# Scaling q and k in place through a tree of block factors in an HGRN2 mixer, and writing TensorE's order in both mixers out by hand

## The chip, the cores and the metric

The kernel runs on one core of a Trainium2 chip. The metric is the time of one execution on the device, in microseconds (us). A core has TensorE (PE; its weight loads are listed as PEld), VectorE (DVE), ScalarE (ACT), GpSimd (POOL) and SyncE (SP, which here only issues transfers). Each engine takes its own instructions in the order in which they stand in its queue, and an instruction that waits for another engine holds up all that stands behind it in its queue.

## The reference

A trunk of four layers over 256 positions of 1024 values. Layers 0 and 3 mix the positions by differential attention, layer 1 by a gated recurrence (HGRN2), layer 2 by a gated MLP. Behind its mixer every layer attends to 256 memory positions and runs a feed-forward block. Cut to the two mixers:

```python
def diff_attention(h, ...):
    q, k, v = jnp.split(h @ w_in, 3, axis=-1)      # 8 heads, 2 x 64 for q and k, 128 for v
    logits = einsum('bqhcd,bkhcd->bhcqk', q, k) * scale + bias, -inf above the diagonal
    p = softmax(logits)
    attn = p[:, :, 0] - lam * p[:, :, 1]
    o = einsum('bhqk,bkhd->bqhd', attn, v)
    return (rmsnorm(o, subln_g) * (1.0 - lam_init)) @ w_out

def hgrn2(h, ...):
    q, f, i, g = jnp.split(h @ w_in, 4, axis=-1)   # 8 heads of 128
    log_f = log(lb + (1 - lb) * sigmoid(f))        # the decay of each position
    key = 1.0 - exp(log_f); qf = silu(q)
    # A[t, s] = sum_k qf[t,k] key[s,k] * (product of the decays of s+1 .. t at k), s <= t
    o = A @ i
    return (rmsnorm(o, onorm_g) * silu(g)) @ w_out
```

## The kernel before

All products with weights are made of three matmuls, since fp32 operands are split into a high and a low part. SP loads weights into three buffers (`wraw`); ScalarE casts the high part (`whi`, line 127), VectorE subtracts it to get the low part (`wlo`, line 128), three units ahead of TensorE's use. `columns_block` writes products transposed, 256 output columns (a unit, 32 matmuls in 16 pairs of lines 197 and 201) at a time, for q, k and HGRN's f; `join` (lines 212 and 213) adds its two halves on ScalarE and VectorE and frees two of the four accumulator banks of PSUM. `rows_block` (line 159) makes v and g. Four further banks (`ps`) are shared by everything small.

In the attention, for each of four head pairs: the logits (line 529), bias and maximum (534, 538), the exps (544), a factor `dco` from the sums (550, 551), the difference `de` (554), and its transposes for the product with v (559, 562). A head pair needs the unit of q of its number. In layer 0 `memory()` also loads and normalises the memory (lines 384 to 394) and transposes it (`pst`, 239) into `m`. In HGRN a triangle of 256 positions is cut into levels of doubling blocks: for each level GpSimd multiplies keys by decay products (`ke`, line 696) and extends these (`hs`, 703), VectorE does the like for q (`qe`, 693, and 700), TensorE multiplies them (`psa`, 715 and 726), and VectorE copies the level's blocks into the triangle `A` by a mask (717). The levels' masks hold the diagonal too.

What sets the order: the Python loops issue everything in program order, and a scheduler then places the instructions on each engine's queue as it expects operands to come. So TensorE's attention and levels lie among the projections where the scheduler puts them.

## Time and profile before

| | |
|---|---|
| median of 3 runs | 1650.75 us (1649.39 to 1651.85) |
| the profiled execution | 1651.97 us, span 1650.3 us |
| PE busy | 1614.3 us, 98% |
| DVE, ACT, POOL busy | 1035.8 us (63%), 875.0 us (53%), 83.8 us (5%) |
| layer 0's attention, first logits to last output matmul | 73.92 to 121.87 |
| HGRN, first diagonal matmul to the end of the levels | 483.15 to 531.63 |
| layer 3's attention | 1286.59 to 1331.46 |

A matmul's row in the timeline carries the time to its modelled end, which overlaps the next one's start; its pace is the difference of two starts. An "x" and a number says how many of a kind follow one another. A bracket at the end of a row gives the idle time before it, and what ended it. In names, an arrow points from the inputs to the output.

### The profile page before, as it was taken

The numbers are of one execution on the slowest core, as the hardware profiler recorded it, in microseconds if no ns is written. First come the engines' busy times: TensorE is split into PE (matmuls) and PEld (weight loads), VectorE is DVE, ScalarE is ACT, GpSimd is POOL, SyncE is SP. The second block draws the span as 40 slices with busy tenths as digits, with TensorE's granted clock in tenths as the row PEclk, the third lists the DMA queues.
The fourth block names the chain that finished last, engine by engine and source line by source line (L and its number), as shares of the span: only waits on it lengthen the run. The fifth ranks groups of instructions, "written<-read, shape, count | busy, mean of one in ns | idle before, by whom it ended". The sixth has DMA issues, their size and how long they took to land.

```text
span 1650.3 us, 21291 instructions
## 1 busy us (share of the span) xinstructions
PE 1614.3 (98%) x8221; PEld 1358.9 (82%) x8221; DVE 1035.8 (63%) x1466; ACT 875.0 (53%) x1451; POOL 83.8 (5%) x104
## 2 busy tenths in 40 slices
PE   7799999999998999999999999999999999999998
PEld 6678888888887888888888888888888788888886
DVE  6687665554689567655545866555547876655453
ACT  5576554453552666554436556544435675554452
POOL 2000000000037000000000000000000000000000
PEclk9899999999999999999999999999999999999999
DMA  8644445546640655455565654555656445455461
GB/s 271 211 134 153 155 153 187 193 164 202 185 141 28 204 178 171 145 193 167 195 213 166 193 185 148 164 179 165 217 182 202 143 138 179 143 184 195 130 233 71
DMA packets 151291, 283.04 MB, mean 172 GB/s; under 512 B 6267, under 2 KB 79894, under 8 KB 151062
## 3 DMA queue, kind: packets, MB, share of 16 engines
q1 hardware_dynamic: 146384, 274.82, 50.7%
q10 hardware_dynamic: 4806, 6.87, 1.4%
q8 instruction: 64, 1.05, 0.3%
q14 instruction: 37, 0.30, 0.1%
HBM read 280.60 MB, written 2.63 MB: 172 GB/s over the span
## 4 chain that ended last, share of the span: by engine, by line
PE 85%; DVE 5%; POOL 3%; ACT 3%; DMA 2%; issue 2%; POOLq 0%; DVEq 0%; ACTq 0%
PE acc L159 63%; PE acc L197 10%; PE acc L201 5%; PE pst L239 3%; PE pso L889 1%; PE psl L850 1%; DVE wlo L128 1%; POOL ke L696 1%; POOL hs L703 1%; ACT de L544 1%; DMA mem<-in_mem_dram 1%; PE pl L529 1%; ACT junk L262 1%; ACT whi L127 1%; DMA x<-in_x_dram 1%
## 5 line engine op out<-in xcount | busy, mean ns | idle before, releaser
L128 DVE TENSOR_TENSOR wlo<-wraw,whi 128x1024 fp32r<-128x1024 f32 (+1 forms) x536 | 637.4, 1196 | 457.2 <-ACT whi L127 453.8
L127 ACT CAST whi<-wraw 128x1024 fp32r<-128x1024 f32 (+1 forms) x536 | 547.3, 1026 | 535.2 <-PE acc L159 464.2
L159 PE MATMUL acc<-whi,xs 128*128 128x512 f32 x1728 | 542.9, 392 | 0.7 <-DVE hf L213 0.7
L159 PEld LDWEIGHTS acc<-whi,xs 128*128 128x128 f32 x1728 | 324.1, 188 | 69.0 <-DVE hf L213 1.5
L159 PE MATMUL acc<-wlo,xs 128*128 128x512 f32 x864 | 337.9, 391 | 0.0
L197 PE MATMUL acc<-xs,whi 128*128 128x512 f32 x704 | 248.8, 398 | 0.0
L201 PE MATMUL acc<-xs,wlo 128*128 128x256 f32 x704 | 196.9, 283 | 0.0
L159 PEld LDWEIGHTS acc<-wlo,xs 128*128 128x128 f32 x864 | 162.4, 188 | 33.2 <-issue 1.0
L197 PEld LDWEIGHTS acc<-xs,whi 128*128 128x128 f32 x704 | 132.4, 189 | 29.0
L159 PE MATMUL acc<-wlo,hh 128*128 128x512 f32 x352 | 137.3, 390 | 0.0
L159 PE MATMUL acc<-whi,hh 128*128 128x512 f32 x352 | 137.3, 392 | 0.0
L201 PEld LDWEIGHTS acc<-xs,wlo 128*128 128x128 f32 x704 | 133.8, 190 | 0.9
L159 PE MATMUL acc<-whi,hl 128*128 128x512 f32 x352 | 111.9, 390 | 0.0
L159 PE MATMUL acc<-whi,oh 128*128 128x512 f32 x256 | 100.2, 391 | 1.7 <-DVE bt L213 1.7
L159 PE MATMUL acc<-wlo,oh 128*128 128x512 f32 x256 | 100.5, 393 | 0.0
L197 PE MATMUL acc<-m,whi 128*128 128x512 f32 x256 | 90.3, 395 | 0.0
L159 PE MATMUL acc<-whi,ol 128*128 128x512 f32 x256 | 84.8, 392 | 0.0
L159 PE MATMUL acc<-whi,m 128*128 128x512 f32 x256 | 80.7, 391 | 0.0
L159 PEld LDWEIGHTS acc<-whi,hh 128*128 128x128 f32 x352 | 66.1, 188 | 14.5 <-DVE ftmp L916 1.1
L159 PEld LDWEIGHTS acc<-whi,hl 128*128 128x128 f32 x352 | 66.1, 188 | 13.7
L159 PEld LDWEIGHTS acc<-wlo,hh 128*128 128x128 f32 x352 | 66.1, 188 | 13.4
L201 PE MATMUL acc<-m,wlo 128*128 128x256 f32 x256 | 72.1, 282 | 0.0
(223 smaller groups left out, 1760.9 us busy)
## 6 DMA issues: line engine op xcount, KB each, us to landing
wraw<-in_ffn_w_gu_dram SPq DMA_DIRECT2D x160, 512.0 KB, 4.5
wraw<-in_ffn_w_down_dram SPq DMA_DIRECT2D x44, 1024.0 KB, 4.9
wraw<-in_ca_w_kv_dram SPq DMA_DIRECT2D x32, 1024.0 KB, 5.2
wraw<-in_da_w_in_dram SPq DMA_DIRECT2D x24, 1024.0 KB, 6.9
wraw<-in_ca_w_q_dram SPq DMA_DIRECT2D x16, 1024.0 KB, 5.2
wraw<-in_ca_w_o_dram SPq DMA_DIRECT2D x16, 1024.0 KB, 4.9
wraw<-in_hg_w_in_dram SPq DMA_DIRECT2D x16, 1024.0 KB, 5.5
wraw<-in_da_w_out_dram SPq DMA_DIRECT2D x8, 1024.0 KB, 4.9
```

The source lines that it names most:

```text
L127: nc.scalar.copy(h, rq)
L128: nc.vector.tensor_tensor(l, rq, h.bitcast(F32), op=ALU.subtract)
L159: nc.tensor.matmul(acc[key], lhsT=x_(k)[:, t * P : (t + 1) * P], rhs=w_[kk][:, 0, c], start=first and j == 0, stop=last and j == 2,)
L197: nc.tensor.matmul(acc[j].rearrange("p (s t) -> p s t", s=2), lhsT=wh[k // 4][:, k % 4, c], rhs=x[:, :, k, :], start=k == 0, stop=False, s ...
L201: nc.tensor.matmul(acc[j][:, 0:256], lhsT=wl[k // 4][:, k % 4, c], rhs=x[:, 0, k, :], start=False, stop=k == 7, skip_group_check=True,)
L239: nc.tensor.transpose(ps[:, i * 256 + t * P : i * 256 + (t + 1) * P], src[:, t, cs * P : (cs + 1) * P], self.ident)
L262: self.nc.scalar.activation(junk[:, : src.shape[1]], src, AF.Square, accum_out=acc)
L529: nc.tensor.matmul(lg[c][:, i * w : (i + 1) * w], lhsT=qt[r, 2 * hp + i, t * P : (t + 1) * P], rhs=kt[r, 2 * hp + i, 0:w], start=True, sto ...
L544: nc.scalar.activation(e[t][:, c, i], e[t][:, c, i], AF.Exp, bias=mx[:, t, k : k + 1], accum_out=sm[:, t, c, i : i + 1])
L696: nc.gpsimd.tensor_tensor(kev[:, :, 0, :], kv[:, :, 0, :], sv[:, :, 0, :], op=ALU.mult)
L703: nc.gpsimd.tensor_tensor(sv[:, :, 0, :], sv[:, :, 0, :], sv[:, :, 1, 0:1].to_broadcast([P, 4 * nb, half]), op=ALU.mult)
L850: nc.tensor.matmul(ps[:, t * 256 : (t + 1) * 256], lhsT=q_[:, 2 * h + d, t * P : (t + 1) * P], rhs=k_[:, 2 * h + d, :], start=n == 0, stop ...
```

## The change

Four things are done.

1. The blocks become generators (`columns_steps`, `rows_steps`) that yield behind each matmul; `advance(filler, n)` issues n more of them. In the mixers, a written list says after how many projection matmuls each piece of attention (`weigh`: logits to `de`; `turn`: its transposes) or each level stands, and `in_order()` makes TensorE keep this order. The other engines are still placed by the scheduler.
2. In HGRN, `hks` holds the key times the next position's decay, and it and q are multiplied in place, level by level, with a tree of block products `bl` (`hb` in the trace) on VectorE. GpSimd's products, `qe`, `ke` and the copy of f are gone.
3. The diagonal is made apart: 16 matmuls of one column each (`psd`) sum q times key, and ScalarE scales the identity by them into `A`.
4. The masks lose their diagonal.

The functions named `weigh` and `turn` have the bodies of the former loop.

```diff
-        self.columns_block(self.xs, done_q)
...
-        for hp in range(4):
+
+        def both():
+            yield from self.columns_steps(self.xs, done_q)
+            yield from self.rows_steps(xh, xl, 8, done_v)
+
+        filler = both()
+        order = self.in_order()
+        order.__enter__()
+
+        def weigh(hp):
...
+            return e
+
+        def turn(hp, e):
+            hs = slice(2 * hp, 2 * hp + 2)
...
-        self.rows_block(xh, xl, 8, done_v)
+        es = {}
+        for n, act, hp in (
+            (44, weigh, 0), (24, weigh, 1), (24, turn, 0), (16, weigh, 2),
+            (20, turn, 1), (12, weigh, 3), (24, turn, 2), (24, turn, 3),
+        ):
+            advance(filler, n)
+            if act is weigh:
+                es[hp] = weigh(hp)
+            else:
+                turn(hp, es.pop(hp))
+        advance(filler, 224)
+        order.__exit__(None, None, None)
...
-            nc.vector.tensor_scalar(kk[:, 2 * b : 2 * b + 2, :], fs, -1.0, 1.0, op0=ALU.mult, op1=ALU.add)
-            nc.vector.tensor_copy(sx[:, 2 * b : 2 * b + 2, 0:255], fs[:, :, 1:256])
+            c = slice(2 * b, 2 * b + 2)
+            nc.vector.tensor_scalar(kk[:, c, :], fs, -1.0, 1.0, op0=ALU.mult, op1=ALU.add)
+            nc.vector.tensor_tensor(ks[:, c, 0:255], kk[:, c, 0:255], fs[:, :, 1:256], op=ALU.mult)
+            nc.vector.tensor_tensor(qk[:, c, :], q[:, c, :], kk[:, c, :], op=ALU.mult)
...
-        self.columns_block(self.xs, done_f)
-
-
-
-        qes = self.slab(4, [P, 2, 8, P], name="qe")
-        ke = self.slab(13, [P, 8, 256], name="ke")
...
-        nc.gpsimd.memset(A, 0.0)
-        nc.gpsimd.memset(f.rearrange("p h (b s) -> p (h b) s", s=2)[:, :, 0:1], 1.0)
-        first = lambda x: x.rearrange("p h (t n) -> p h t n", t=2)[:, :, :, 0]
...
-        ps = self.ps("psd")
-        nc.tensor.matmul(ps[:, 0:16], lhsT=self.ones, rhs=qk.rearrange("p h t -> p (h t)"), start=True, stop=True)
-        nc.scalar.copy(A[0:1, :, :, 0].rearrange("p t h -> p h t"), ps[0:1, 0:16].rearrange("p (h t) -> p h t", h=8))
-        for lev in range(8):
...
+        def diagonal(hq):
+            ps = self.ps("psd")
+            dg = self.small([P, 8], "hdg", bufs=2)
+            for i in range(4):
+                for t in range(2):
+                    nc.tensor.matmul(
+                        ps[:, 2 * i + t : 2 * i + t + 1], lhsT=qk[:, hq * 4 + i, t * P : (t + 1) * P],
+                        rhs=self.ones[:, 0:1], start=True, stop=True,
+                    )
+            nc.vector.tensor_copy(dg, ps[:, 0:8])
+            for i in range(4):
+                for t in range(2):
+                    nc.scalar.mul(A[:, t, hq * 4 + i, :], self.ident, dg[:, 2 * i + t : 2 * i + t + 1])
...
+            if lev == 0:
+                f2 = f[:, hs, 1:255].rearrange("p h (b s) -> p h b s", s=2)
+                nc.vector.tensor_tensor(bl[1][:, hs, 0:127], f2[:, :, :, 0], f2[:, :, :, 1], op=ALU.mult)
+            else:
+                b2 = bl[lev][:, hs].rearrange("p h (b s) -> p h b s", s=2)
+                nc.vector.tensor_tensor(bl[lev + 1][:, hs], b2[:, :, :, 0], b2[:, :, :, 1], op=ALU.mult)
+            ps = self.ps("psa")
+            for t in range(2):
+                for i in range(4):
+                    h = hq * 4 + i
+                    o = t * 256 + i * 64
+                    right = q[:, h, t * P : (t + 1) * P].rearrange("p (b s e) -> p b s e", s=2, e=half)[:, :, 1, :]
...
-                nc.gpsimd.tensor_tensor(kev[:, :, 0, :], kv[:, :, 0, :], sv[:, :, 0, :], op=ALU.mult)
...
-                        nc.vector.tensor_tensor(
-                            fv[:, :, 1, :], fv[:, :, 1, :], sv[:, :, 0, 0:1].to_broadcast([P, 4 * nb, half]), op=ALU.mult
...
-                    nc.gpsimd.tensor_tensor(
-                        sv[:, :, 0, :], sv[:, :, 0, :], sv[:, :, 1, 0:1].to_broadcast([P, 4 * nb, half]), op=ALU.mult
...
+            else:
+                for x, s in ((qv, 1), (kv, 0)):
+                    flat = x.rearrange("p h b s e -> p (h b) s e")[:, :, s, :]
+                    by = bl[lev][:, hs].rearrange("p h (b s) -> p (h b) s", s=2)[:, :, 1 - s : 2 - s]
+                    nc.vector.tensor_tensor(flat, flat, by.to_broadcast([P, 4 * nb, half]), op=ALU.mult)
...
+        def both():
+            yield from self.columns_steps(self.xs, done_f)
+            yield from self.rows_steps(xh, xl, 8, done_v)
+            yield from self.rows_steps(xh, xl, 8, done_g)
+
+        filler = both()
+        with self.in_order():
+            advance(filler, 88)
+            diagonal(0)
+            advance(filler, 12)
+            level(0, 0)
+            advance(filler, 22)
+            level(1, 0)
+            advance(filler, 30)
+            diagonal(1)
+            advance(filler, 8)
+            for i in range(14):
+                level(*((i // 2, 1) if i % 2 == 0 else (2 + i // 2, 0)) if i < 12 else (i - 6, 1))
+                advance(filler, 9 if i < 11 else 17)
+            advance(filler, 320)
```

The step that lets the other blocks run between:

```diff
@@ -198,13 +221,17 @@
                         acc[j].rearrange("p (s t) -> p s t", s=2), lhsT=wh[k // 4][:, k % 4, c], rhs=x[:, :, k, :],
                         start=k == 0, stop=False, skip_group_check=True,
                     )
+                    yield
                     nc.tensor.matmul(
                         acc[j][:, 0:256], lhsT=wl[k // 4][:, k % 4, c], rhs=x[:, 0, k, :],
                         start=False, stop=k == 7, skip_group_check=True,
                     )
+                    if k < 7 or j == 0:
+                        yield
             if mid is not None and u == at:
                 mid()
             done(u, acc)
+            yield
```

TensorE in layer 0, before, around the transposes of the memory (`pst<-ident,mem`) and q's projection (`acc`), of which 83 matmuls stand ahead of the first transpose:

```order
L197 MATMUL acc<-xs,whi 128x512
L201 MATMUL acc<-xs,wlo 128x256
L197 MATMUL acc<-xs,whi 128x512
L239 MATMUL pst<-ident,mem 128x128 x4
L201 MATMUL acc<-xs,wlo 128x256
L197 MATMUL acc<-xs,whi 128x512
L239 MATMUL pst<-ident,mem 128x128 x12
L201 MATMUL acc<-xs,wlo 128x256
L197 MATMUL acc<-xs,whi 128x512
L201 MATMUL acc<-xs,wlo 128x256
```

The same place after the change; 44 matmuls of q stand ahead, and the first logits (`pl`) directly behind:

```order
L220 MATMUL acc<-xs,whi 128x512
L225 MATMUL acc<-xs,wlo 128x256
L220 MATMUL acc<-xs,whi 128x512
L225 MATMUL acc<-xs,wlo 128x256
L266 MATMUL pst<-ident,mem 128x128 x16
L563 MATMUL pl_606<-dk,dq 128x128
L563 MATMUL pl_607<-dk,dq 128x128
L563 MATMUL pl_606<-dk,dq 128x128
L563 MATMUL pl_607<-dk,dq 128x128
L563 MATMUL pl_619<-dk,dq 128x256
L563 MATMUL pl_620<-dk,dq 128x256
L563 MATMUL pl_619<-dk,dq 128x256
L563 MATMUL pl_620<-dk,dq 128x256
```

The transposes moved up by 39 matmuls, and stand as one piece between q's first part and the logits.

ScalarE in layer 0, before, from the load of the memory to its squares (`junk`):

```order
L384 DMA mem<-in_mem_dram 128x2x1024
L127 CAST whi<-wraw 128x1024
L212 COPY dq<-acc 128x256 x2
L127 CAST whi<-wraw 128x1024
L262 ACTIVATE junk,ss<-mem 128x512
L127 CAST whi<-wraw 128x1024
L262 ACTIVATE junk,ss<-mem 128x512
L212 COPY dq<-acc 128x256
```

And after; `bias<-tbd` is the load of the attention's bias:

```order
L411 DMA mem<-in_mem_dram 128x2x1024
L641 DMA bias<-tbd 128x8x256
L289 ACTIVATE junk,ss<-mem 128x512
L131 CAST whi<-wraw 128x1024
L289 ACTIVATE junk,ss<-mem 128x512
L239 COPY dq<-acc 128x256
L289 ACTIVATE junk,ss<-mem 128x512
L239 COPY dq<-acc 128x256
```

The casts and joins between the memory's load and its first use moved behind that use, and the bias load ahead of it.

VectorE in layer 3, before, through the first head pair's softmax (`dq<-acc,dq` is a join of q):

```order
L213 TENSOR_TENSOR dq<-acc,dq 128x256
L534 SCALAR_TENSOR_TENSOR de<-pl_10613,dsc,bias 128x256
L534 SCALAR_TENSOR_TENSOR de<-pl_10614,dsc,bias 128x256
L213 TENSOR_TENSOR dq<-acc,dq 128x256
L538 TENSOR_REDUCE dmx<-de 128x4
L534 SCALAR_TENSOR_TENSOR de<-pl_10626,dsc,bias 128x512
L534 SCALAR_TENSOR_TENSOR de<-pl_10627,dsc,bias 128x512
L128 TENSOR_TENSOR wlo<-wraw,whi 128x1024
L538 TENSOR_REDUCE dmx<-de 128x4
L128 TENSOR_TENSOR wlo<-wraw,whi 128x1024
L548 COPY ds_10609<-dsm 128x4
L608 RECIPROCAL hrs<-ds_10609 128x4
```

And after the change, through the same softmax and the next joins:

```order
L572 TENSOR_REDUCE dmx<-de 128x4
L568 SCALAR_TENSOR_TENSOR de<-pl_10522,dsc,bias 128x512
L568 SCALAR_TENSOR_TENSOR de<-pl_10523,dsc,bias 128x512
L572 TENSOR_REDUCE dmx<-de 128x4
L582 COPY ds_10431<-dsm 128x4
L657 RECIPROCAL hrs<-ds_10431 128x4
L584 RECIPROCAL dco<-dsm 128x4
L585 SCALAR_TENSOR_TENSOR dco<-dco,lam,ds_10431 128x4
L240 TENSOR_TENSOR dq<-acc,dq 128x256
L588 SCALAR_TENSOR_TENSOR de<-de,dco 128x128 x2
L588 SCALAR_TENSOR_TENSOR de<-de,dco 128x256 x2
L240 TENSOR_TENSOR dq<-acc,dq 128x256
```

Two joins of q moved from ahead of the softmax to behind `dco`, the second also behind the four updates of `de`, and the weight subtractions from inside the softmax to behind it.

VectorE in HGRN, before, at the end of the f block and the first level:

```order
L658 TENSOR_SCALAR hk<-hf 128x512
L659 COPY hs<-hf 128x2x255
L680 TENSOR_TENSOR qk<-hq,hk 128x16
L128 TENSOR_TENSOR wlo<-wraw,whi 128x1024
L693 TENSOR_TENSOR qe<-hq,hf 128x512
L717 COPY_PREDICATED hA<-masks,psa 128x256 x2
L700 TENSOR_TENSOR hf<-hf,hs 128x256x2
L717 COPY_PREDICATED hA<-masks,psa 128x256 x2
L717 COPY_PREDICATED hA<-masks,psa 128x128x2 x2
L693 TENSOR_TENSOR qe<-hq,hf 128x512 x2
```

And after, in the f block's third quarter, where the block factors (`hb`) and the products for the diagonal (`hqk`) are made:

```order
L721 TENSOR_TENSOR hqk<-hq,hk 128x512
L712 TENSOR_TENSOR hf<-hf,rb 128x512
L132 TENSOR_TENSOR wlo<-wraw,whi 128x1024
L715 TENSOR_SCALAR hf<-hf,lb 128x256 x2
L132 TENSOR_TENSOR wlo<-wraw,whi 128x1024
L719 TENSOR_SCALAR hk<-hf 128x512
L760 TENSOR_TENSOR hb<-hf 128x4x127
L720 TENSOR_TENSOR hks<-hk,hf 128x2x255
L721 TENSOR_TENSOR hqk<-hq,hk 128x512
L763 TENSOR_TENSOR hb<-hb 128x256
L742 COPY hdg<-psd 128x8
```

The products with f moved from the levels into the f block's own time, between the weight subtractions.

## Rows read from the trace of the kernel before

**Rows 1.** The page: the span, and TensorE's busy time, its share and instructions.
```profile
span 1650.3 us, 21291 instructions
...
PE 1614.3 (98%) x8221; PEld 1358.9 (82%) x8221; DVE 1035.8 (63%) x1466; ACT 875.0 (53%) x1451; POOL 83.8 (5%) x104
```

**Rows 2.** TensorE's waits: line, releaser, total us, times, longest.
```profile
PE pst L239 <- DVE mem L394: 9.5, 1, 9.5
PE pst L239 <- DMA x<-in_x_dram: 5.8, 3, 4.0
```

**Rows 3.** Windows: stretch, length, busy us of PE, PEld, DVE, ACT, POOL, clock, DMA.
```profile
73.90:121.90 48.00, 47.48 (x279) 38.31 (x278) 39.87 (x76) 36.37 (x112) 1.01 (x1) 1.00 0.47 150
483.00:531.60 48.60, 43.56 (x303) 37.99 (x301) 47.76 (x57) 10.36 (x20) 42.20 (x29) 1.00 0.03 10
1286.60:1331.50 44.90, 43.40 (x256) 34.46 (x255) 37.54 (x72) 35.34 (x109) 1.01 (x1) 1.00 0.39 128
```

**Rows 4.** Timeline of TensorE in layer 0: start, us, line, operation [idle <-releaser].
```profile
38.11 0.40 PE L197 MATMUL acc<-xs,whi 128*128 128x512 f32 x1
...
51.98 0.40 PE L197 MATMUL acc<-xs,whi 128*128 128x512 f32 x1
...
61.85 1.11 PE L239 MATMUL pst<-ident,mem 128*128 128x128 f32 x4 [9.47 <-DVE mem L394]
...
62.62 0.56 PE L201 MATMUL acc<-xs,wlo 128*128 128x256 f32 x1
```

**Rows 5.** Timeline of TensorE in layer 3's attention.
```profile
1286.59 1.58 PE L529 MATMUL pl<-dk,dq 64*128 64x128 f32 x16
...
1289.13 0.85 PE L159 MATMUL acc<-whi,xs 128*128 128x512 f32 x3
...
1290.50 0.84 PE L159 MATMUL acc<-whi,xs 128*128 128x512 f32 x3
...
1297.17 1.87 PE L529 MATMUL pl<-dk,dq 64*128 64x128 f32 x16
```

**Rows 6.** Timeline of TensorE at the start of HGRN's levels.
```profile
483.15 0.37 PE L682 MATMUL psd<-qk,ones 128*128 128x16 f32 x2
483.37 1.98 PE L715 MATMUL psa<-hq,ke 128*128 128x64 f32 x16
485.15 0.48 PE L159 MATMUL acc<-whi,xs 128*128 128x512 f32 x1
```

**Rows 7.** Timeline of ScalarE around the memory's load; ACTq marks a DMA issue.
```profile
42.47 0.41 ACTq L384 DMA_DIRECT2D mem<-in_mem_dram  x1
...
55.79 0.63 ACT L262 ACTIVATE junk<-mem 128x512 bf16<-128x512 f32 x1 [10.34 <-DMA mem<-in_mem_dram]
...
64.92 0.47 ACT L228 ACTIVATE m<-pst,G 128x256 fp32r<-128x256 f32 x1 [0.17 <-PE pst L239]
```

**Rows 8.** Timeline of SyncE: weight loads issued in that time.
```profile
46.16 18.97 SPq L111 DMA_DIRECT2D wraw<-in_da_w_in_dram  x3
```

**Rows 9.** Timeline of VectorE behind the memory's normalisation.
```profile
62.37 2.35 DVE L128 TENSOR_TENSOR wlo<-wraw,whi 128x1024 fp32r<-128x1024 f32 x2
```

**Rows 10.** Timeline of VectorE in layer 3: a join, and the softmax's end.
```profile
1288.13 0.42 DVE L213 TENSOR_TENSOR dq<-acc,dq 128x256 f32<-128x256 f32 x1
...
1294.86 0.18 DVE L550 RECIPROCAL dco<-dsm 128x4 f32<-128x4 f32 x1 [0.60 <-ACT de L544]
...
1295.34 1.41 DVE L554 SCALAR_TENSOR_TENSOR de<-de,dco 128x128 f32<-128x128 f32 x4
```

**Rows 11.** Timeline of VectorE in HGRN's f block: one line twice.
```profile
468.36 0.68 DVE L652 TENSOR_TENSOR hf<-hf,rb 128x512 f32<-128x512 f32 x1
...
473.32 1.57 DVE L652 TENSOR_TENSOR hf<-hf,rb 128x512 f32<-128x512 f32 x1
```

**Rows 12.** Windows with TensorE's clock: after the two longest waits (columns as rows 3).
```profile
12.00:14.00 2.00, 2.00 (x9) 1.70 (x9) 1.95 (x2) 1.62 (x5) 0.00 (x0) 1.00 1.06 347
58.00:66.00 8.00, 4.15 (x19) 3.97 (x20) 6.45 (x11) 6.04 (x13) 0.70 (x1) 0.50 0.45 134
```

More of the change, by code (lines that the diff above doesn't have):

```diff
@@ L59, in level_masks, with advance @@
         t = np.array([t for t in range(P) if t // half % 2 == 1])[None, :]
-        left = (s // (2 * half) == t // (2 * half)) & (s // half % 2 == 0)
-        out.append(left | ((s == t) & (t % half == 0)))
+        out.append((s // (2 * half) == t // (2 * half)) & (s // half % 2 == 0))
     return np.ascontiguousarray(np.stack(out, 1).astype(np.float32))
+def advance(gen, n):
+    for _ in range(n):
+        next(gen, None)
 class Trunk:
@@ L139, in next_unit, with rows_block, in_order, rows_steps @@
         return self.spl.pop(i)
-    def rows_block(self, xh, xl, nk, done, width=1024, tmajor=False, mid=None, at=None):
+    def rows_block(self, *args, **kw):
+        for _ in self.rows_steps(*args, **kw):
+            pass
+    def in_order(self):
+        return self.tc.manual_schedule(engines={mybir.EngineType.PE})
+    def rows_steps(self, xh, xl, nk, done, width=1024, tmajor=False, mid=None, at=None):
         nc = self.nc
@@ L171, in rows_block @@
                     for n in range(nn):
-                        mm((t, n), k, kk, wh, wl, (0, 1))
+                        for j in range(2):
+                            mm((t, n), k, kk, wh, wl, (j,))
+                            yield
                     for n in range(nn):
                         mm((t, n), k, kk, wh, wl, (2,))
+                        yield
         if mid is not None and at is None:
@@ L180, in rows_block, with columns_block, columns_steps @@
                 for kk in range(2):
-                    mm(key, 2 * (nu - FIN + i) + kk, kk, wh, wl, (0, 1, 2))
+                    for j in range(3):
+                        mm(key, 2 * (nu - FIN + i) + kk, kk, wh, wl, (j,))
+                        if not (j == 2 and kk == 1 and i == FIN - 1):
+                            yield
             done(*key, acc.pop(key))
-    def columns_block(self, x, done, width=1024, mid=None, at=2):
+            yield
+    def columns_block(self, *args, **kw):
+        for _ in self.columns_steps(*args, **kw):
+            pass
+    def columns_steps(self, x, done, width=1024, mid=None, at=2):
         nc = self.nc
@@ L200, in columns_block @@
                     )
+                    yield
                     nc.tensor.matmul(
@@ L207, in columns_block @@
             done(u, acc)
+            yield
     def join(self, out, banks):
@@ L637, in hgrn2 @@
         kk = self.slab(11, [P, 8, 256], name="hk")
-        sx = self.slab(12, [P, 8, 256], name="hs")
+        ks = self.slab(12, [P, 8, 256], name="hks")
         v = self.slab(14, [P, 2, D], name="hv")
         g = self.slab(3, [P, 2, D], name="hg")
-        nc.gpsimd.memset(sx[:, :, 255:256], 1.0)
+        qk = self.slab(4, [P, 8, 256], name="hqk")
+        A = self.slab(7, [P, 2, 8, P], name="hA")
+        A01 = self.slab(8, [P, 8, P], name="hA01")
+        blocks = self.slab(13, [P, 8 * 254], name="hb")
+        bl, o0 = {}, 0
+        for e in range(1, 8):
+            n = 256 >> e
+            bl[e] = blocks[:, o0 : o0 + 8 * n].rearrange("p (h b) -> p h b", h=8)
+            o0 += 8 * n
+        nc.gpsimd.memset(ks[:, :, 255:256], 0.0)
+        nc.gpsimd.memset(bl[1][:, :, 127:128], 1.0)
         def done_v(t, n, ps):
@@ L685, in hgrn2, with level @@
+        def level(lev, hq):
+            hs = slice(hq * 4, hq * 4 + 4)
+            if lev == 7:
+                ps = self.ps("psa")
+                for i in range(4):
+                    h = hq * 4 + i
+                    nc.tensor.matmul(ps[:, i * P : (i + 1) * P], lhsT=ks[:, h, 0:P], rhs=q[:, h, P:256], start=True, stop=True)
+                nc.scalar.copy(A01[:, hs, :], ps.rearrange("p (h t) -> p h t", h=4))
+                return
             half = 1 << lev
             nb = P // half
-            qe = qes[:, lev % 2]
@@ new lines, in level @@
+            for t in range(2):
+                for i in range(4):
+                    h = hq * 4 + i
+                    o = t * 256 + i * 64
+                    right = q[:, h, t * P : (t + 1) * P].rearrange("p (b s e) -> p b s e", s=2, e=half)[:, :, 1, :]
+                    nc.tensor.matmul(
+                        ps[:, o : o + 64].rearrange("p (b e) -> p b e", e=half),
+                        lhsT=ks[:, h, t * P : (t + 1) * P], rhs=right, start=True, stop=True,
+                    )
@@ new lines, in level @@
+            for t in range(2):
+                nc.vector.copy_predicated(
+                    A[:, t, hs, :].rearrange("p h (b s e) -> p h b s e", s=2, e=half)[:, :, :, 1, :],
+                    self.masks[:, lev, :].rearrange("p (b e) -> p b e", e=half).unsqueeze(1).to_broadcast([P, 4, nb // 2, half]),
+                    ps[:, t * 256 : (t + 1) * 256].rearrange("p (h b e) -> p h b e", h=4, e=half),
+                )
+        def both():
+            yield from self.columns_steps(self.xs, done_f)
+            yield from self.rows_steps(xh, xl, 8, done_v)
+            yield from self.rows_steps(xh, xl, 8, done_g)
```

47 lines of the change are left out of this document (7 added, 40 removed).

## The prediction

> **What bounds the kernel now.** I read the page first: TensorE is busy for 1614.3 of 1650.3 us [rows 1]. The profiled execution took 1651.97 us, 1.7 more than its span; the median of the three timed runs is 1650.75. I count from 1651.97 and round at the end. So the time moves only by what the change puts on TensorE's own stream: more passes, or waits. Second I read the list of TensorE's waits: the one large wait is 9.5 us for the memory's normalised tiles in layer 0; the next is for x, at the program's start [rows 2]. Third, the windows of the three mixer stretches [rows 3]: 48.00 us in layer 0, 44.90 in layer 3 and 48.60 in HGRN, where VectorE is busy for 47.76 and GpSimd for 42.20. TensorE's "busy" there includes slack that its ends are modelled with, so I price the work by start-to-start paces instead.
>
> Paces: a column-projection matmul 0.1734 us (38.11 to 51.98 is 80 of them) [rows 4]; a row-projection matmul 0.228 (1289.13 to 1290.50 is six) [rows 5]; one pass of a small fp32 matmul 0.11 (483.15 to 483.37 is two, 483.37 to 485.15 is sixteen) [rows 6]; the 16 logit passes of the first head pair about 1.5 (1.58 less what overlaps), 0.3 more for later ones (1.87) [rows 5].
>
> **What waits and fragments cost before.** Layer 0's stretch issues 96 row matmuls (21.8), 46 column matmuls (8.0), 64 logit passes (6.0), 24 transposes (2.6) and 48 output passes (5.3): 43.8 of 48.0, so 4.2 us are lost. Layer 3 has 23 column matmuls: 39.8 of 44.9, 5.1 lost. HGRN has 59 row matmuls (13.4), 14 groups of 16 passes (24.9), 16 passes of level 7 (1.8) and the first diagonal (0.2): 40.4 of 48.5, 8.1 lost. The windows of rows 3 are these stretches to 0.1 us.
>
> **Part A, the memory's transposes (worse by 3.8).** Before, TensorE runs 83 of q's matmuls, to 51.98, and stands until 61.85 [rows 4]. In the changed order the 16 transposes stand right behind the 44th. TensorE comes there at 38.11 + 42 x 0.1734 = 45.4, and 39 matmuls (6.8 us) that lay beside the wait come behind it. What ends the wait is a chain: ACT issues the memory's load at 42.47, and uses it first at 55.79 [rows 7]. Meanwhile SP's queue started weight loads at 46.16 [rows 8]. In the new ACT order the cast of the weights follows the memory's first use, so the buffer that SP waits for stays full, and that load no longer shares the flight; the bias load now stands behind the memory's on the same queue. I take 3.0 us off, near the 1 MB that leaves the flight; ends 0 (the bias takes its place) and 4.0 (all of it). A: 6.8 - 3.0 = +3.8, from +2.8 to +6.8.
>
> **Part B, layer 0's first logits (worse by 2.1).** They stand directly behind the 16 transposes and need PSUM banks that are emptied by eight pairs of m operations, at one pair per 0.64 us (64.92 is one, 0.47 on ACT with 0.17 idle before it) [rows 7], on VectorE behind two weight subtractions of together 2.35 [rows 9]. Eight pairs are 5.1 us, 16 transposes some 3.1 at the pace of 62.62 less 61.85 for four: 2.0, plus a hand-over of 0.1. Ends 0 (banks return in time) and 3.0.
>
> **Part C, second logits (worse by 6.9).** This is the largest term. The logits of head pair 1 need q's unit 1, whose two joins on VectorE now stand behind head pair 0's softmax: one behind `dco`, the other behind four `de` updates. Before, they stood ahead of it. From layer 3's rows: logits start at 1286.59 [rows 5]; `dco` starts at 1294.86, when the last exp lets it, and the four updates start at 1295.34 and take 1.41; a join takes 0.42 [rows 10]. Start to end that is 10.2 us and 0.8 more for two joins. I take off 1.4 for what the two weight subtractions and the old joins between those steps held up: the second join ends about 9.6 us behind the logits' start. TensorE arrives after 1.5 + 24 x 0.1734 = 5.7. Wait: +3.6 in layer 3; in layer 0, where the table load is not in the chain, +3.3. Ends: 0 (if the exps overlap more) and 4.5 each.
>
> **Parts D and E (worse by 3.3 and 4.2).** Head pair 2's logits need unit 2's join in the same way, but come 24 + 16 matmuls and a turn later: 1.45 in layer 0 and 1.85 in layer 3 remain. The fourth accumulator of v waits for unit 3's second join behind `dco` of pair 2: 2.1 in each layer. Each runs from 0 to twice its value.
>
> **Part F, gains in attention (better by 5.3).** The 4.2 + 5.1 us of lost time go with the order that caused them; 1.1 us per layer of switches between projections and attention stay, and 0.9 per layer of the slower later logits (3 x 0.3): 9.3 - 4.0 = 5.3.
>
> **Part G, HGRN (worse by 3.7).** GpSimd's key and decay products go, and so does what they do to VectorE: line 652 took 0.68 us alone and 1.57 beside GpSimd [rows 11]. The 8.1 lost us go; 17 returns to the projections stay, each some 0.12, since the first matmul behind another kind is longer (0.48 at 485.15 [rows 6], against 0.39 for one of the three that take 0.85 in rows 5): 2.0. So -6.1. The Trainium skill (SBUF — State Buffer, section Who interferes with whom) says that a VectorE instruction with two SBUF inputs is fully blocked by a GpSimd instruction that reads SBUF; the trace agrees, 1.57 against 0.68 us, and by that rule alone the part would be a gain of 6.1. What it leaves out is what is added: the diagonal has 16 one-column matmuls of two passes, 32 against 2 before, 30 x 0.11 = +3.3. The same notes (TensorE: Matmul & The Clock Gate, section Back-to-back issue gap) list some 25 ns for a matmul of 1 to 64 columns; by it this would be 0.8 and the sum 2.5 lower, but the row with 16 columns has 0.11 a pass and decides. Waits added: the first diagonal needs `hqk` of unit 1. From that unit's last matmul TensorE needs 24 x 0.1734 = 4.2 us to come there; VectorE has two weight subtractions (2.35 [rows 9]), five products of 512 elements (0.6 to 0.68 each [rows 11]), two joins (0.8) and some 1.5 of small ones to do, 7.7: +3.5. By the same count v's first accumulators wait 1.6 for hf's last joins, the second diagonal 1.45. In the 14 level steps TensorE has 16 x 0.11 + 9 x 0.228 + 0.12 = 3.9 us and VectorE two scalings (0.6 each), a weight subtraction (1.2) and two predicated copies of half the elements (0.35 each, an estimate from the scalings), 3.1: no wait. If that cover went (1.57 for each scaling, as in the disturbed row) VectorE would have 5.0, 1.1 us a step, 15 in all. Sum: -6.1 + 3.3 + 3.5 + 1.6 + 1.45 = +3.7, from -3 to +11.
>
> Scaling q and k in place adds 28 VectorE operations but takes out as many, and the identity products go to ACT, which waits for TensorE there; both cost nothing beside TensorE. The sum: 3.8 + 2.1 + 6.9 + 3.3 + 4.2 - 5.3 + 3.7 = +18.7, 1651.97 + 18.7 = 1670.7; I write 1670.
>
> **The rivals.** *The clock falls in the new waits.* After 9.47 us of nothing the granted clock was 0.50 for eight us [rows 12], the 1.2 GHz level; in the 4.0 us wait for x at the start [rows 2] it was 1.00 right behind it [rows 12]. If the three waits of 3.3 to 3.6 us each cost some 2.5 us at the low level, and layer 0 stays low longer, the time is 1670 + 7.5 + 0.5 = 1678. For it: layer 0's wait gets longer; against it: the 4.0 us row. Chance 0.12.
>
> *VectorE and ACT run ahead.* D, E (7.5) vanish and half of G's waits (3.2) because the joins are reached earlier than I counted: 1670.7 - 10.7 = 1660. For it: each term rests on one queue position and 1 to 2 us. Chance 0.24.
>
> *Faster.* One mechanism: the joins of q are reached on VectorE before the softmax chain's exps end, because the weight subtractions taken out between them give it up to 2.4 us per head pair, so none of B to E waits, and hqk comes in time too. Then 1652 + 3.8 - 5.3 - 6.1 + 3.3 = 1647.7. It decides when the second join ends within 5.7 us of the logits' start; my chain is 9.6, and `dco` alone starts at 8.3 in the rows. Chance 0.12.
>
> *No change.* The gains of F and G meet waits of 13 instead of 25 us: about 1652. That includes the case that the written order does what the scheduler's did anyway. Chance 0.06.
>
> **How the numbers follow.** My forecast, 1664 to 1676 around 1670, has 0.46. A difference under 0.2% (3.3 us) can't be told from none here. Faster 0.12, within 0.2% 0.06, slower 0.46 + 0.24 + 0.12 = 0.82. For 8 in 10 I leave out the faster case and half of no change (0.15) and a small end above: 1652 to 1681. The likeliest case's own range is 1664 to 1676.
>
> **What would show it.** A: the wait of pst at line 266 grows from 9.5 to about 13. C: a wait of pl at line 563 of 3 to 4 us on `dq`, once per attention layer, and shorter ones for D; E: acc waits on `dq` of 2 us. G: psd waits on `hqk` for 3.5, its 16 passes take 1.8 us in each half, and GpSimd's rows at HGRN are gone; the level steps come every 3.9 us. I am wrong if pl shows no wait on `dq`, if level steps wait for VectorE, or if the diagonal's passes are far below 0.11.

## The result and the profile after

The changed kernel takes 1669.49 us (median of 4, 1668.92 to 1671.77) against 1650.07 (4 runs): a ratio of 1.0116, 95% interval 1.0103 to 1.0128. The forecast was 1670. The profiled execution's span grew from 1650.3 to 1669.8 us.

The page of the changed kernel answers to [rows 1], its list of TensorE's waits (line, releaser, total us, times, longest) to [rows 2]:

```profile
span 1669.8 us, 21300 instructions
...
PE 1620.5 (97%) x8251; PEld 1368.5 (82%) x8251; DVE 1025.4 (61%) x1487; ACT 874.2 (52%) x1452; POOL 35.9 (2%) x73
```

```profile
PE pst L266 <- DVE mem L421: 12.8, 1, 12.8
PE pl L563 <- DVE dq L240: 6.3, 5, 1.9
PE psd L738 <- DVE hqk L721: 5.8, 2, 3.9
...
PE acc L171 <- DVE dq L240: 2.9, 2, 1.5
PE acc L171 <- DVE hf L240: 1.9, 1, 1.9
...
PE pl L563 <- DVE m L256: 0.9, 1, 0.9
```

TensorE is busy for 6.2 us more, and the waits that the prediction named are there: the memory's normalised tiles now hold the transposes for 12.8 us instead of 9.5; the logits wait 6.3 us for joins of q, the diagonals 5.8 us for `hqk`, v's first matmuls 2.9 and 1.9, the first logits 0.9 for `m`. Waits for GpSimd's `ke` are no longer in the list; before the change they were two of its lines, 4.3 us together:

```profile
PE psa L715 <- POOL ke L696: 2.5, 4, 0.7
...
PE psa L726 <- POOL ke L696: 1.8, 2, 1.3
```

To see where the 19.5 us of span lie, take starts that both kernels have: layer 0 from the last gain transpose (psg) to the next layer block's first transpose of x, HGRN and layer 3 from the row sums (psr) to that transpose.

| stretch | before | after | change | forecast |
|---|---|---|---|---|
| start of the program to the last psg | 37.50 | 36.99 | -0.5 | 0 |
| layer 0's attention and what follows | 121.83 | 131.45 | +9.6 | +10.5 |
| HGRN | 166.15 | 173.40 | +7.25 | +3.7 |
| layer 3's attention | 126.58 | 129.80 | +3.2 | +4.5 |
| everything else | | | +0.0 | 0 |

The table compares one execution of each kernel, and that of the changed kernel is the longest of its four. Three of the later runs keep the changed attention code: there layer 0 lies 6.1 to 7.6 us above the kernel before, and layer 3 4.3 to 4.5 (a fourth run that keeps it in layer 3 has 3.1). Two keep the changed HGRN code: +6.9 and +7.3. So the row of HGRN is firm, and those of the attentions are good to some 3 and 1 us.

The forecast's sum is right to 1 us, but HGRN is 3.5 us worse than forecast, and layer 0 is better. The reason for HGRN is in the windows with the granted clock (columns as rows 3), which answer to [rows 12]:

```profile
62.00:64.00 2.00, 2.00 (x10) 1.65 (x8) 2.00 (x5) 1.67 (x4) 0.00 (x0) 0.50 0.00 0
66.00:68.00 2.00, 2.00 (x13) 1.37 (x12) 1.80 (x5) 0.47 (x1) 0.00 (x0) 0.50 0.82 332
...
480.00:482.00 2.00, 0.00 (x0) 0.00 (x0) 2.00 (x4) 0.00 (x0) 0.00 (x0) 1.00 0.94 258
482.00:483.00 1.00, 0.03 (x1) 0.03 (x1) 1.00 (x3) 0.00 (x0) 0.00 (x0) 0.79 0.98 406
484.00:488.00 4.00, 4.00 (x14) 3.52 (x15) 1.32 (x7) 2.92 (x10) 0.00 (x0) 0.50 0.00 0
488.00:490.00 2.00, 2.00 (x14) 1.90 (x12) 1.48 (x3) 0.99 (x2) 0.00 (x0) 0.65 0.00 0
510.00:512.00 2.00, 2.00 (x7) 1.62 (x7) 0.61 (x4) 1.65 (x6) 0.00 (x0) 0.50 0.90 276
```

Where the column says 0.50 TensorE is busy throughout, and at 1.2 GHz (in 488 to 490 it came back to 2.4 GHz). At the first diagonal the fall lies in the wait itself: the window from 482 to 483, in which TensorE stands but for 0.03 us, already has 0.79. Its timeline there, which answers to [rows 6], shows the wait and the price (here and below, the count of a `psd` row is of passes, two to a matmul):

```profile
478.11 0.95 PE L738 MATMUL psd<-ones,hqk 128*128 128x1 f32 x8
482.97 1.87 PE L738 MATMUL psd<-ones,hqk 128*128 128x1 f32 x8 [3.92 <-DVE hqk L721]
484.70 0.77 PE L220 MATMUL acc<-xs,whi 128*128 128x512 f32 x1
...
485.49 0.63 PE L220 MATMUL acc<-xs,whi 128*128 128x512 f32 x1
...
488.69 2.24 PE L770 MATMUL psa<-hq,hks 128*128 128x64 f32 x16
```

The second half of the first diagonal waits 3.92 us; behind it a high-part column matmul's row is 0.63 to 0.77 us long against 0.40 in [rows 4], and the twelve projection matmuls from 484.70 to 488.69 take 3.99 us instead of 12 x 0.1734 = 2.1. VectorE's queue in layer 3, which answers to [rows 10], shows the forecast order at work:

```profile
1289.23 0.88 DVE L568 SCALAR_TENSOR_TENSOR de<-pl,dsc,bias 128x256 f32<-128x256 f32 x2 [0.58 <-PE pl L563]
...
1295.54 0.18 DVE L584 RECIPROCAL dco<-dsm 128x4 f32<-128x4 f32 x1 [0.60 <-ACT de L578]
...
1295.89 0.42 DVE L240 TENSOR_TENSOR dq<-acc,dq 128x256 f32<-128x256 f32 x1
1296.23 1.40 DVE L588 SCALAR_TENSOR_TENSOR de<-de,dco 128x128 f32<-128x128 f32 x4
1297.54 0.41 DVE L240 TENSOR_TENSOR dq<-acc,dq 128x256 f32<-128x256 f32 x1
1297.87 1.21 DVE L132 TENSOR_TENSOR wlo<-wraw,whi 128x1024 fp32r<-128x1024 f32 x1
```

The join of the second unit's first half starts behind `dco`, the other one behind the four updates, and ends 9.9 us behind the logits' start at 1288.09. The forecast had 9.6.

### The profile page after: what moved, and what is told of

It reads as the page before. It is cut to its first block, busy times and chain, and to the rows that moved or that the text cites. A ratio compares the mean times of both kernels' runs of the same rounds, so it can differ in the third digit from the quotient of the medians.

```text
span 1669.8 us, 21300 instructions
## 1 busy us (share of the span) xinstructions
PE 1620.5 (97%) x8251; PEld 1368.5 (82%) x8251; DVE 1025.4 (61%) x1487; ACT 874.2 (52%) x1452; POOL 35.9 (2%) x73
## 5 line engine op out<-in xcount | busy, mean ns | idle before, releaser
L220 PE MATMUL acc<-xs,whi 128*128 128x512 f32 x704 | 254.0, 404 | 1.8 <-DVE dk L240 1.8
```

Source lines behind the costliest of these rows:

```text
L220: nc.tensor.matmul(acc[j].rearrange("p (s t) -> p s t", s=2), lhsT=wh[k // 4][:, k % 4, c], rhs=x[:, :, k, :], start=k == 0, stop=False, s ...
```

## The experiments

**One part alone.** In `hgrn_alone` the attention's function is the former one again; in `attention_alone` the kernel before gets the generators and the attention's written order, and HGRN's function and masks stay the former ones. The first of the two against the changed kernel:

```diff
+        self.columns_block(self.xs, done_q)
...
-        filler = both()
-        order = self.in_order()
-        order.__enter__()
-
-        def weigh(hp):
+        for hp in range(4):
...
-        advance(filler, 224)
-        order.__exit__(None, None, None)
+        self.rows_block(xh, xl, 8, done_v)
```

> The changed HGRN with its written order; both attentions as before. My theory (the loss is made of waits that the written order puts on TensorE, and of its clock falling to 1.2 GHz in them, each in its own stretch, so the stretches add): from the traces, HGRN's stretch between the norms around it got 7.2 us longer, so 1650 + 7 = 1657, with psd waits of 3.9 and 1.9 us on hqk and a granted clock of 0.5 behind them, as in the changed kernel. Rival (the attention's changed end shifts what HGRN finds, or the algebra alone is a gain): within 2 us of 1650 or below.

> The attentions in the written order; HGRN as before. My theory: layer 0 lost 9.6 us and layer 3 3.2 by the traces, so 1650 + 13 = 1663; together with the run of the changed HGRN alone the two losses add to the whole, 19 to 20. Rival (one of the losses is shared or moved between stretches): the two do not add within 3 us.

Measured: 1658.04 us (ratio 1.0044, 1.0029 to 1.0059) and 1662.13 (1.0071, 1.0056 to 1.0086) against 1650.47. The losses are 7.6 and 11.7 us, together 19.2 of 19.4: each part is slower by itself, and they add. The waits are those of the whole (psd 5.8 us in the one; pl 6.1, pst 13.6 in the other).

**The scheduler's order again.** TensorE is no longer held to the written order; the algebra, the generators and the lists stay:

```diff
-        return self.tc.manual_schedule(engines={mybir.EngineType.PE})
+        return nullcontext()
```

> The changed algebra and the changed program text, but TensorE's order in the mixers is left to the scheduler. My theory (order, not algebra): the memory's transposes come behind some 83 matmuls of q again and the joins ahead of the softmaxes, and HGRN has no key products on GpSimd; 1650 - 8.1 + 2 + 3.3 = about 1647, within 1643 to 1653. Rival (the algebra itself costs VectorE too much in the f block, which sets the pace there): the psd waits of about 4 us stay and the time is 1655 or more.

Measured: 1640.43 us (0.9939, 0.9922 to 0.9955), 29 us less than with the written order, 10 less than before the change, and below the range I had given. The list of its waits has none of `psa` or `psd`, so the 4.3 us that TensorE stood for `ke` before the change are gone, and with them most of what HGRN gained. VectorE is quicker too, as two groups of its operations between 440 and 600 us show. Before (line, operation, tile, count, then busy us and mean ns):

```profile
L693 DVE TENSOR_TENSOR qe<-hq,hf 128x512 f32<-128x512 f32 x14 | 19.9, 1453 | 0.0
L700 DVE TENSOR_TENSOR hf<-hf,hs 128x512 f32<-128x512 f32 x12 | 14.3, 1215 | 0.0
```

and in this run, where the in-place products take their place:

```profile
L783 DVE TENSOR_TENSOR hq<-hq,hb 128x512 f32<-128x512 f32 x12 | 8.2, 683 | 4.6 <-PE psa L770 4.6
L783 DVE TENSOR_TENSOR hks<-hks,hb 128x512 f32<-128x512 f32 x12 | 8.2, 682 | 0.0
```

With GpSimd's products beside them, those of 512 elements took 1453 and 1215 ns on average, without them 683. The HGRN stretch is 160.50 us against 166.15, and TensorE is busy in all of 482 to 530 at a clock of 1.00. So part G's gain was there, larger than the 2.8 that the forecast's terms without waits add up to (-6.1 + 3.3), and the written order spent it; how much of it is VectorE's speed and how much GpSimd's place in the chain was not taken apart. Layer 0 (119.37 against 121.83) and layer 3 (123.12 against 126.58) are shorter too.

**The same lists with later numbers.**

```diff
-            (44, weigh, 0), (24, weigh, 1), (24, turn, 0), (16, weigh, 2),
+            (68, weigh, 0), (28, weigh, 1), (24, turn, 0), (14, weigh, 2),
...
-            advance(filler, 88)
+            advance(filler, 112)
             diagonal(0)
-            advance(filler, 12)
+            advance(filler, 8)
...
-            advance(filler, 30)
+            advance(filler, 36)
             diagonal(1)
...
-                advance(filler, 9 if i < 11 else 17)
+                advance(filler, 9)
```

> The changed kernel with other numbers in its two lists: the first logits (and with them the memory's transposes) stand behind 68 instead of 44 matmuls of q, each head pair's logits so far back that the unit of q it needs was finished one step earlier, and both diagonals 24 and 30 projection matmuls later. My theory: layer 0 gets back 4.2 us of matmuls beside the memory's wait and some 4 of waits, layer 3 about 7 (waits 5.8, clock 1.8), HGRN about 10 (psd 5.8, hf 1.9, clock 3): 1669.5 - 25 = about 1645, from 1640 to 1652, and no wait of psd or pl above 1 us. Rival (VectorE's and ScalarE's rate is the bound, so the waits come back at the transposes of de or at the levels): 1658 to 1668, with waits of pat on de or psa on hq or hks instead.

Measured: 1643.35 us (0.9958, 0.9943 to 0.9972). Against the table's execution layer 0 got back 9.8 us, layer 3 8.4, HGRN 10.9. What is left of the waits:

```profile
PE acc L220 <- DVE dq L240: 6.2, 1, 6.2
...
PE pl L563 <- DVE m L256: 2.5, 2, 1.5
PE acc L171 <- DVE hf L240: 1.5, 1, 1.5
PE pst L266 <- DVE mem L421: 1.1, 1, 1.1
```

No wait of psd, none of pl for dq; one for `m` is above the 1 us of the expectation (1.5). The 6.2 us of acc are what was the memory's wait: TensorE stands in front of a later unit of q until 54.33, for a join that comes on VectorE behind a weight subtraction, whose cast comes on ScalarE behind the memory's first use at 51.02. The rival's waits on `de` and on the levels are absent: the rate of VectorE and ScalarE was not the bound, the queue position was.

**Is the slow clock the wait's doing?** TensorE is given work in the waits, matmuls of 512 columns into a bank that nothing reads:

```diff
+            self.keep_busy(16)
             diagonal(0)
...
+            self.keep_busy(7)
             diagonal(1)
```

> The changed kernel with 16 and 7 more row-sized matmuls, into a bank that nothing reads, in front of the two diagonals, where TensorE waits 3.9 and 1.9 us for hqk: 3.6 and 1.6 us of work that lies in the waits. Theory (the fall of the clock to 1.2 GHz behind such a wait is a cost of its own): the granted clock stays at 1.00 in the windows from 482 to 490 and 510 to 514, the 12 projection matmuls behind the first diagonal take 2.1 instead of 4.0 us and the HGRN stretch gets 4 to 5 us shorter, 1665. Rival (the wait alone is the cost): 1669 to 1670, the stretch within 1 us.

Measured: 1670.27 us (1.0121, 1.0106 to 1.0136), the HGRN stretch 172.89 against 173.40. The gain that the theory asked for did not come. The waits for `hqk` shrank from 5.8 to 1.5 us in all, filled with work, and the clock fell all the same:

```profile
478.00:480.00 2.00, 2.00 (x12) 1.67 (x10) 2.00 (x4) 0.00 (x0) 0.00 (x0) 1.00 0.83 246
482.00:484.00 2.00, 2.00 (x10) 1.76 (x10) 1.13 (x6) 1.69 (x6) 0.00 (x0) 0.78 0.00 0
484.00:486.00 2.00, 2.00 (x10) 1.81 (x9) 0.76 (x2) 2.00 (x6) 0.00 (x0) 0.50 0.00 0
508.00:510.00 2.00, 2.00 (x7) 1.61 (x7) 0.27 (x2) 1.23 (x5) 0.00 (x0) 0.50 0.26 107
```

It fell later and for a shorter time: at the first diagonal it is low from 483.1 to 486.5, where the changed kernel has 482.6 to 489.4; at the second both have it low for 3.4 us. The first fall comes 1.2 us behind the diagonal's 16 one-column passes, with TensorE never idle for more than 0.25 us there, so no wait of some length is needed for it. The second still stands behind a wait of 1.29 us. That a run of such passes is enough by itself is not shown either, since the kernel with the later lists has the same 16 passes at a stretch in both of these windows, with no wait ahead of them, at full clock:

```profile
470.00:480.00 10.00, 9.88 (x67) 8.67 (x65) 8.73 (x18) 6.34 (x15) 0.00 (x0) 1.00 0.57 205
492.00:500.00 8.00, 8.00 (x53) 7.19 (x52) 5.21 (x12) 4.00 (x10) 0.00 (x0) 1.00 0.75 260
```

The same trial in layer 0 (there the memory's transposes are also issued inside the written order, so that they stand behind the added matmuls):

```diff
             advance(filler, n)
+            if l == 0 and n == 44:
+                self.keep_busy(54)
+                turn_memory()
```

> The changed kernel with 54 more row-sized matmuls in front of the memory's transposes in layer 0, 12.3 us of work in a wait of 12.8. Theory: the clock stays at 1.00, the 16 transposes take 1.7 instead of 3.7 us, the first logits 1.5 instead of 4.0, and the wait of the second logits for dq, 1.1 us in the changed kernel, comes out at about the 3.3 of the prediction, since TensorE arrives earlier; the chain through VectorE bounds what is gained, so the whole gets 3 us shorter, 1666.5. Rival (the slow clock there is hidden by VectorE's chain altogether): 1669 to 1670.

Measured: 1670.86 us (1.0122, 1.0106 to 1.0139). Layer 0's stretch was 2.2 us shorter, but runs that leave layer 0 as it is were 2.0 to 3.5 us shorter than that execution too, so none of it is shown to come from the added work, and the time shows no gain. The clock held through the filled wait (still 1.00 in 62 to 64) and then fell behind the transposes, a wait of 2.1 us for `m` and the logits' start (0.50 in 66 to 68), so the second logits' wait stayed at 1.1.

The new theory, that a run of one-column passes lowers the clock, is tested by spreading the passes. First, the busy kernel with the diagonals cut into pairs:

```diff
             for i in range(4):
+                if i:
+                    advance(filler, 4)
                 for t in range(2):
...
-            advance(filler, 12)
             level(0, 0)
...
-            advance(filler, 30)
+            advance(filler, 26)
+            self.keep_busy(7)
             diagonal(1)
-            advance(filler, 8)
```

> The changed kernel with the 16 and 7 row-sized matmuls in the two waits for hqk, as in the run that kept TensorE busy in them, and each diagonal's eight matmuls in four pairs with four projection matmuls between the pairs, which take the place of those that stood behind the diagonal. In that run the clock fell all the same, behind the diagonals. Theory (a solid run of one-column passes lowers the clock, beside or without an idle wait): no stretch of HGRN below 1.00 behind the diagonals; its length, 173.4 in the changed kernel and 172.9 in the busy run, comes to 169 to 170; the kernel to 1666. Rival (the fall comes from something else at that place): 0.50 behind the diagonals again and 172 to 173.5.

Measured: 1665.57 us (1.0094, 1.0079 to 1.0109); HGRN 168.06 us. The clock now holds:

```profile
478.00:480.00 2.00, 2.00 (x16) 1.82 (x16) 1.81 (x4) 0.00 (x0) 0.00 (x0) 1.00 0.76 311
480.00:482.00 2.00, 2.00 (x18) 1.87 (x16) 0.75 (x3) 1.61 (x3) 0.00 (x0) 1.00 0.00 0
482.00:484.00 2.00, 2.00 (x18) 1.96 (x19) 1.85 (x5) 1.77 (x6) 0.00 (x0) 1.00 0.00 0
484.00:486.00 2.00, 2.00 (x13) 1.78 (x12) 2.00 (x4) 0.74 (x4) 0.00 (x0) 1.00 0.73 180
500.00:506.00 6.00, 6.00 (x43) 5.43 (x42) 3.89 (x10) 3.47 (x9) 0.00 (x0) 1.00 0.36 108
```

Against the busy run the same number of passes and matmuls is 4.8 us shorter; pairing also lets the last `hqk` come later, which removes the remaining waits of 1.5, so some 3.3 us are the clock. That fits the 6.8 us that the busy run spent at half the clock. Since the waits went together with the solid run, the second diagonal doesn't say which of the two lowers the clock; at the first, where the wait was 0.25 us, it is hardly the wait. Second, the price of a pass, on the kernel with later lists: each diagonal matmul three times, at a stretch and in groups.

```diff
-                for t in range(2):
+                for t in (0, 0, 0, 1, 1, 1):
```

The second of the two runs has, besides that, the following, and fewer projection matmuls around the diagonals and the first two levels, in place of those that now stand between the groups:

```diff
+                    if spread and n % 4 == 0 and n:
+                        advance(filler, 4)
+                    n += 1
```

> The kernel with the later lists, each of the 16 diagonal matmuls issued three times (the same result): 32 more one-column matmuls, 64 more passes. By the row of before at 0.11 us a pass, which the prediction took: 1643.35 + 7.0 = 1650. By the page's 25 ns for a matmul of 1 to 64 columns: 64 passes would be 1.6, 1645.

> The kernel with the later lists and each diagonal matmul issued three times, as in the run that took 1657.15, but in groups of four matmuls (eight passes) with four projection matmuls between the groups. Theory (64 passes cost 0.107 each, 6.8 us, and the rest of the 13.8 us that they added was the clock): the clock stays at 1.00, ten more returns to projections at 0.12, 1643.35 + 6.8 + 1.2 = 1651.4. Rival (a one-column pass costs 0.2 us in such numbers whatever the clock does): 1657 again, at a clock of 1.00 if the clock has no part.

Measured: 1657.15 us (1.0041, 1.0026 to 1.0056) and 1654.57 (1.0031, 1.0020 to 1.0043). At a stretch, 64 passes cost 13.8 us, twice the 7.0 by the row and far above the 1.6 by the other price; timeline of that run at the first diagonal and behind it:

```profile
474.33 6.03 PE L738 MATMUL psd<-ones,hqk 128*128 128x1 f32 x48
...
481.00 0.63 PE L220 MATMUL acc<-xs,whi 128*128 128x512 f32 x1
481.43 0.41 PE L225 MATMUL acc<-xs,wlo 128*128 128x256 f32 x1
481.64 0.63 PE L220 MATMUL acc<-xs,whi 128*128 128x512 f32 x1
```

The 48 passes take 5.88 us (the next matmul starts at 480.21), 0.12 each, and the matmuls behind them run at the low pace (0.43 and 0.21 from start to start, where rows at full clock have 0.23 and 0.12). In groups a pass takes 0.10:

```profile
474.73 0.95 PE L741 MATMUL psd<-ones,hqk 128*128 128x1 f32 x8
475.54 0.48 PE L220 MATMUL acc<-xs,whi 128*128 128x512 f32 x1
...
476.32 0.95 PE L741 MATMUL psd<-ones,hqk 128*128 128x1 f32 x8
```

Eight passes from 474.73 to 475.54. The clock is 1.00 from 470 to 490 in that run, but the second level met a wait of 2.6 us for `hks` that the shifted list made, and 490 to 500 shows 0.83: the clock is low from 493.0 to 496.4, behind that wait and 9 us behind the last one-column passes. Without the wait the run is at 1652.0, against an expected 1651.4, and without the 3.4 us at half the clock some 1.7 lower still.

**A faster version.** The scheduler's order in layer 0 and HGRN, the later list in layer 3; then, on top, the memory's load ahead of the constants' loads, into a buffer that waits for nothing:

```diff
-        order = self.in_order()
+        order = self.in_order() if l else nullcontext()
...
+            (68, weigh, 0), (28, weigh, 1), (24, turn, 0), (14, weigh, 2),
+            (20, turn, 1), (12, weigh, 3), (24, turn, 2), (24, turn, 3),
+        ) if l else (
...
-        with self.in_order():
+        with nullcontext():
```

```diff
-        g1 = self.slab(3, [P, P], name="g1b")
+        g1 = self.slab(4, [P, P], name="g1b")
...
         if l == 0:
+            self.mem = self.slab(3, [P, 2, D], name="mem")
+            nc.scalar.dma_start(out=self.mem, in_=...)
             self.more_consts()
```

> A version that joins what was shorter: the scheduler's order in layer 0 and HGRN with the changed algebra, the later list in layer 3. Stretches add: layer 0 119.4 and HGRN 160.5 as with the scheduler's order, layer 3 121.4 as with the later list, against 123.1: 1640.4 - 1.7 = 1638.7. Rival (layer 3's gain hangs on what lies ahead of it): 1640 or more.

> The version with the scheduler's order and layer 3's list, and the memory's load issued ahead of the constants' loads, into a buffer that no longer waits for the gains (these go through another). Theory (what bounds layer 0's middle is the landing of the memory): the 8.1 us of waiting around the memory's transposes shrink to the next bound, the bias, which must pass through DRAM first; layer 0's stretch 119.9 to some 115, the kernel 1634. Rival (the load takes its bandwidth from the first weights, which TensorE waits for at the start): no gain or up to 3 us worse.

Measured: 1638.90 us (0.9931, 0.9916 to 0.9946) and 1637.12 (0.9921, 0.9906 to 0.9936). The first has the stretches that were to add (119.9, 160.5, 121.4), and comes out 0.2 us from the expected sum. In the second layer 0's stretch fell from 119.9 to 116.6, and the start grew from 37.1 to 38.8 us, which gives back half. Whether the load did that is not shown, since the other runs' starts lie between 36.1 and 38.1. The memory is in use at 35.2 now, but TensorE still waits 6.9 us for its normalised tiles: ScalarE stands for 4.1 us until 46.99 in front of the bias table's issue, behind which the memory's last two squares lie, while GpSimd copies that table. Both beat the kernel before and the changed one; the last is the fastest.

## Why the prediction was right

The mechanism, waits of TensorE at the places of the written list, held; that the sum came out to 1 us is luck, as the parts below show.

**The bound and the method** held: TensorE's stream sets the time, and the 1198 us outside the four stretches of the table did not move by 0.1 us.

**A**, forecast +3.8: the transposes stand behind 44 matmuls and start at 60.36, 1.5 us earlier than before and not 3.0, so A is 6.8 - 1.5 = 5.3 by this execution, inside its range. The flight of the memory did get shorter, 13.3 to 9.9 us from issue to use, with SP's queue silent until 57.23 as argued; but the issue was 1.95 us later (44.42), since the copy of the bias table ahead of it on that queue went out at 43.65 instead of 41.51. That delay is not the change's: `hgrn_alone`, with the former attention, has the copy at 42.17. In the three other runs with the changed attention the transposes start 1.8 to 4.6 us earlier than before, counted from the last psg (1.0 here), so A lies between 2.2 and 5.8.

**B**, forecast +2.1: 0.9 was seen here, and 2.1 in the run that kept the clock up through the transposes. The agreement of the latter is chance: the 3.1 us that the sum took for 16 transposes come from a row at 61.85 [rows 4], in a window at the low clock [rows 12], and at full clock 15 of them have 1.86 us.

**C, D, E**, forecast 6.9, 3.3 and 4.2: the places were right, the sizes too large. C was 3.1 in layer 3 (1.94 and 1.15) against 3.6 and 1.1 in layer 0 against 3.3; D 0.9 and 1.3 against 1.45 and 1.85; E 1.5 and 1.4 against 2.1. In layer 0 TensorE itself was late: 16 logits took 4.0 us and 24 projection matmuls 6.2 at the low clock, so the join was nearly there. In D and E a wait that has already been taken shifts TensorE, and the next one is shorter; I had priced them as if alone. No run takes these waits apart, so this reason is argued. One wait had no place in the forecast: 1.8 us of q's first accumulators for joins of k, which the changed HGRN with the former attention has too (1.2).

**F and G** without their waits: the scheduler's-order run shows the gain of the algebra (5.6 us in HGRN with the diagonal included), twice the 2.8 of the forecast. F was never seen apart; in layer 3 what is left of the +3.2 without waits (5.8) and slow clock (1.7) is -4.3, where the forecast has -3.1. G's waits were forecast at 6.55 and measured at 5.8 + 1.9 = 7.7. In the 14 level steps TensorE never waited, one step each 3.87 us (forecast 3.9), as the cover of VectorE's 3.1 promised.

**The step that failed** is the one that dismissed the clock: "it was 1.00 right behind it", said of the 4.0 us wait for x at the start. I gave the fall a chance of 0.12 and no place in the sum. In the changed kernel it is there three times outside layer 0: at the first diagonal 0.9 us on its last eight passes, 1.9 on twelve projection matmuls and 0.35 on a level; behind the second 0.5 on nine projection matmuls and 0.9 on a level; in layer 3 1.0 on the second logits and 0.7 on the matmuls behind them. That is 6.3 us. In layer 0 it covers the 12.6 us from the transposes at 60.36 to 73.0, against 5.1 before, which is not in these 6.3. The waits were forecast some 5 us too large and the gains of HGRN and layer 3 together some 3 too small, so errors of both signs left the sum 1 us off, by luck; HGRN, whose waits were not oversized, came out 3.5 us above its forecast. The rival had the fall right and its chance too low. Its cause, the new waits, holds where the fall lies in one (482 to 483) or behind one (layer 3, 1.94 and 1.15 us); but filling the waits didn't hold the clock, and in HGRN spreading the one-column passes did. What lowers it in general stays open.

The 4.0 us row was also misread. The timeline of the kernel before, right behind that wait:

```profile
14.34 0.63 PE L197 MATMUL acc<-xs,whi 128*128 128x512 f32 x1
14.77 0.41 PE L201 MATMUL acc<-xs,wlo 128*128 128x256 f32 x1
...
16.04 0.40 PE L197 MATMUL acc<-xs,whi 128*128 128x512 f32 x1
16.28 0.28 PE L201 MATMUL acc<-xs,wlo 128*128 128x256 f32 x1
```

A high-part matmul takes 0.63 us at 14.34 and 0.40 at 16.04: TensorE ran at half pace there, in a window that says 1.00. The trace of this execution holds no record of the clock before 15.8 us, and the column shows 1.00 where there is none; so the row said nothing of the clock. The paces of matmuls tell it, also where the column does not.

**Diagonal**: 0.10 to 0.107 us a pass at full clock (0.22 at the low one: 482.97 to 484.70 are eight), near the 0.11 taken from the row with 16 columns. The 25 ns that the Trainium skill (TensorE: Matmul & The Clock Gate, section Back-to-back issue gap) lists for 1 to 64 columns, in a table for matmuls by themselves, do not show in any run.

## What to carry to other kernels

When an order is written out for one engine, look up where the scheduler then puts what that engine waits for on the others' queues: here each new wait of over 1 us in layer 3 and HGRN was for a join or product that stood behind a softmax or weight subtractions, and moving the waiting pieces later, the first by 24 matmuls, made those waits of the logits and the diagonals vanish. Price a wait with what follows it, since one taken wait shortens the next. Where the clock falls behind a solid run of tiny matmuls, try breaking the run up with large ones (here worth some 3 us), and read the clock from the start-to-start pace of a known matmul.

## What the runs showed of the hardware

- The granted clock fell to 0.50 behind 16 one-column passes that followed large matmuls, with TensorE idle for 0.25 us at the most; the same passes in groups of four left it at 1.00. In the kernel with later lists the same 16 passes at a stretch did not lower it, and three times as many did (0.95 from 470 to 480, 0.54 from 480 to 490). It also fell in a wait of 3.92 us and behind one of 2.6. What decides between these is open.
- At the start of the program, where the trace has no record of the clock, the column says 1.00 while matmuls run at half pace (0.63 against 0.40 us).
- VectorE's products of 512 elements with both inputs in SBUF took 1453 and 1215 ns beside GpSimd and 683 without it, in the direction that the Trainium skill (SBUF — State Buffer, section Who interferes with whom) gives.
